# Token factors of the feed-forward's first norm applied to the up projection's outputs, with four leading tiles side by side

## The chip, the cores and the metric

The kernel runs on one core of a Trainium2 chip. The metric is the device time of one execution in microseconds (us). A core has five engines that run their own instruction queues in order: TensorE (PE in the profile, its weight loads PEld), VectorE (DVE), ScalarE (ACT), GpSimd (POOL) and SyncE (SP), which issues the loads from memory. They wait for one another by semaphores. TensorE's results land in PSUM, eight banks of 128 x 512 fp32 numbers; everything else lives in SBUF.

## What is computed

Two layers of a hybrid encoder, all in fp32, on 512 tokens of 1024 channels:

```python
def rms_norm(x, g):
    y = xf * lax.rsqrt(jnp.mean(xf * xf, axis=-1, keepdims=True) + RMS_EPS)
    return y * g
...
for l in range(DEPTH):                      # DEPTH = 2
    h = rms_norm(x, g_pre_mix[l])
    proj = h @ w_in[l]                      # 1024 -> 5632
    ...
    merged = (gates[:, :, 0] * (o_a @ w_br_a[l]) + gates[:, :, 1] * (o_b @ w_br_b[l])
              + gates[:, :, 2] * (o_m @ w_br_m[l]))
    x = x + rms_norm(merged @ w_out[l], g_post_mix[l])
    h = rms_norm(x, g_pre_ffn[l])
    u = depthwise_conv_centred(h @ w_up[l], conv_w[l], conv_b[l])   # 1024 -> 5632, 3 taps over tokens
    a, b = jnp.split(u, 2, axis=-1)
    f = jax.nn.gelu(a) * b
    x = x + rms_norm(f @ w_down[l], g_post_ffn[l])
```

The three attention branches o_a, o_b, o_m (the last one into 256 memory tokens) lie between; the change does not touch them. The norm that matters is the one behind `w_out`: it divides every token by one number, the root of the mean of its squares, and multiplies every channel by g.

## The kernel before

**Layout and precision.** Channels lie on the 128 partitions and tokens along the free axis, so x is eight tiles of 128 x 512 (k = 0 to 7). A product is made as three matmuls of a rounded format (`mm3`): each operand is split into a high part (a cast on ScalarE) and a low part (source minus high part, on VectorE or GpSimd), and high x high, high x low and low x high are summed in PSUM. An output tile of 128 channels takes 8 steps over k of 3 matmuls. It is made at full width (24 matmuls of 512 tokens) or by halves (48 of 256), which lets it begin when only the first 256 tokens of its input are there.

**Weights.** `weights()` loads 512 KB through SP's queue into one of three buffers `wraw`, casts it on ScalarE to `whi` and subtracts on VectorE to `wlo` (two buffers each), or into other pools where the weights have to stay longer. Low parts for which GpSimd is named are made there instead.

**Order.** TensorE's order is written out by hand: the class `Woven` chains every matmul to the one before it and keeps a clock of their estimated cost. Side work (norms, attention heads) stands in generators, the jobs, that are woven in when the clock passes their due time. A job yields a delay or the name of a flag that it waits for; the main line waits with `need` and jobs answer with `give`. The order on the other engines is chosen by the framework's scheduler; each engine then runs its queue in that order.

**The stage of the change.** `sublayer_end` makes the output tiles of `w_out` (and later of `w_down`): each is scaled by g on ScalarE into a tile `og`, and its squares are summed into `acc`. For `w_out` all eight tiles are made by halves. When a token half is complete, `end_job` runs: `rstd_job` multiplies the sums by a vector `mean` on TensorE (the tokens' means land on the partitions), takes the root on ScalarE and the reciprocal on VectorE, builds a diagonal matrix from it on VectorE and multiplies it by a matrix of ones on TensorE, so that every partition of a PSUM tile `pr` holds the 256 factors. Then x is updated, its squares are summed, and `pre_norm_job` does the same a second time for the next norm and makes h = x * g * factor with high and low parts. The flag `h{l}.16.i` says that half i of h is complete.

The up projection has 44 output tiles; tile j and tile j + 22 form a pair. The first six (0, 22, 1, 23, 2, 24) lead: their weights are made ahead, with GpSimd's low parts, and `run_group` computes them by halves, two side by side, in six PSUM banks. The other 38 are made at full width, one after another. `conv` reads the tile from PSUM (ScalarE: middle tap and bias; VectorE: two steps with the other taps), then come GELU, the product of the pair and the split for `w_down`. The casts of the first two single tiles are put behind the last operation of the norm on ScalarE (`fence`).

Between the layers, the last norm of layer 0 and the first of layer 1 run beside the projection of the memory tokens (`mem_kv`). At the start of the program and at its end `rstd_job` has little beside it.

In the profile nearly all operations of ScalarE and VectorE carry line 114 (the helper through which they go), matmuls line 244, transposes 255, GpSimd's low parts 222.

## Time and profile before

| | us |
|---|---|
| median of three runs | 1577.96 (1577.94, 1577.96, 1579.77) |
| the profiled execution | 1579.04 |
| its span, first to last instruction | 1577.3 |
| PE busy | 1529.7 |
| DVE busy | 911.2 |
| ACT busy | 727.4 |
| POOL busy | 186.4 |

The profiled execution is 1.7 us longer than its span: that much lies around the first and last instruction. A row of the timeline gives the start, the time to the end of the last of a group of like instructions, the engine, the line, the operation with its output and inputs, their number, and in brackets the idle time of the engine just before them and what ended it. Matmuls are pipelined, so the time of one is the distance of two starts. A row of windows gives, for a stretch of the span, the busy time of the five engines with the number of instructions, then TensorE's granted clock (1.00 is full speed), the share of the DMA engines and GB/s.

### The profile page before, as it was taken

To read this page: it belongs to the slowest core of one execution; us is meant where nothing else is said; L and a number is where in the kernel's file an instruction comes from. 1 tells how busy PE (TensorE), PEld (TensorE's weight loads), DVE (VectorE), ACT (ScalarE), POOL (GpSimd) and SP (SyncE) were. 2 spreads that over 40 slices of the span, in tenths; PEclk is the share of its full clock that TensorE was granted. 3 is DMA by queue.
4 is the path that set the end of the run, shared out by engine and by line. 5 is a ranking of instruction groups with operands and counts; after the bars stand their busy time and mean duration, and the time that the engine had idled before them with its cause. 6 is when DMAs were issued, how large, how long until landed. Compare 5 with 4: busy or idle time off the path is not lost.

```text
span 1577.3 us, 21375 instructions
## 1 busy us (share of the span) xinstructions
PE 1529.7 (97%) x8246; PEld 1316.4 (83%) x8246; DVE 911.2 (58%) x1654; ACT 727.4 (46%) x1289; POOL 186.4 (12%) x244
## 2 busy tenths in 40 slices
PE   6999999999999999999989999999999999999997
PEld 5988888889898888878888888888898888888887
DVE  6686566344866666542386856743457666664233
ACT  5465575334544444532345646733454544444231
POOL 4340000110400000010062300001121000000000
PEclk9999999999999999999999999999999999999998
DMA  7222213224213222333331221132431232223331
GB/s 241 87 78 67 66 56 100 88 94 134 81 42 106 93 95 96 115 97 100 115 113 49 86 69 56 51 120 74 140 101 48 69 105 95 94 96 96 99 103 62
DMA packets 46614, 144.96 MB, mean 92 GB/s; under 512 B 5232, under 2 KB 11376, under 8 KB 46512
## 3 DMA queue, kind: packets, MB, share of 16 engines
q1 hardware_dynamic: 44656, 139.61, 27.7%
q10 hardware_dynamic: 1152, 2.10, 0.5%
q0 software_dynamic: 704, 1.88, 0.4%
q8 instruction: 65, 1.06, 0.3%
q14 instruction: 37, 0.30, 0.1%
HBM read 141.47 MB, written 2.10 MB: 91 GB/s over the span
## 4 chain that ended last, share of the span: by engine, by line
PE 88%; DVE 8%; ACT 2%; issue 1%; DMA 1%; SPq 0%; ACTq 0%
PE mm L244 73%; PE s L244 6%; PE o L244 3%; PE pt L244 2%; DVE h L114 2%; PE pt L255 2%; DVE y L114 2%; DVE x L114 1%; DVE m L114 1%; DVE wlo L114 1%; ACT whi L114 1%; DVE acc L114 1%; DVE ka L114 0%; ACT y L114 0%; DMA m<-in_memT_dram 0%
## 5 line engine op out<-in xcount | busy, mean ns | idle before, releaser
L244 PE MATMUL mm<-h,whi 128*128 128x512 f32 x2432 | 755.7, 392 | 0.0
L244 PEld LDWEIGHTS mm<-h,whi 128*128 128x128 f32 x2432 | 449.6, 188 | 88.7
L114 DVE TENSOR_TENSOR wlo<-wraw,whi 128x1024 fp32r<-128x1024 f32 (+1 forms) x203 | 246.9, 1218 | 394.9 <-ACT whi L114 394.8
L244 PE MATMUL mm<-h,wlo 128*128 128x512 f32 x1216 | 473.9, 390 | 0.0
L114 ACT CAST whi<-wraw 128x1024 fp32r<-128x1024 f32 (+1 forms) x203 | 210.3, 1038 | 296.5 <-PE mm L244 295.7
L244 PEld LDWEIGHTS mm<-h,wlo 128*128 128x128 f32 x1216 | 228.2, 188 | 48.5
L244 PE MATMUL mm<-m,whi 128*128 128x512 f32 (+1 forms) x672 | 178.2, 354 | 1.6 <-DVE m L114 0.8
L244 PEld LDWEIGHTS mm<-m,whi 128*128 128x128 f32 x672 | 119.6, 192 | 19.0 <-PE mm L244 1.3
L114 DVE SCALAR_TENSOR_TENSOR y<-mm,vec,y 128x511 f32<-128x511 f32 x160 | 118.9, 746 | 8.5 <-ACT y L114 5.9
L244 PE MATMUL mm<-m,wlo 128*128 128x512 f32 (+1 forms) x336 | 118.3, 352 | 0.7 <-DVE wlo L114 0.7
L114 ACT ACTIVATE y<-mm,vec 128x512 f32<-128x512 f32 (+1 forms) x163 | 113.6, 698 | 0.1
L244 PE MATMUL mm<-m,m 128*128 128x512 f32 (+1 forms) x432 | 88.6, 346 | 0.0
L222 POOL TENSOR_TENSOR m<-wraw,m 128x512 fp32r<-128x512 f32 x42 | 56.3, 1355 | 238.5 <-ACT m L114 234.2
L728 POOL TENSOR_TENSOR m<-m,y 128x512 f32<-128x512 f32 x28 | 36.1, 1289 | 405.7 <-DVE y L114 405.7
L244 PEld LDWEIGHTS mm<-m,m 128*128 128x128 f32 x432 | 67.6, 190 | 8.4
L244 PEld LDWEIGHTS mm<-m,wlo 128*128 128x128 f32 x336 | 64.4, 192 | 9.4 <-DVE wlo L114 1.1
L114 ACT ACTIVATE y<-y 128x512 f32<-128x512 f32 x44 | 27.8, 632 | 87.3 <-DVE y L114 87.3
L244 PE MATMUL mm<-h,m 128*128 128x256 f32 x456 | 63.6, 296 | 4.0 <-ACT h L114 1.6
L114 DVE TENSOR_TENSOR acc<-acc,sq 128x256 f32<-128x256 f32 (+1 forms) x86 | 44.6, 521 | 37.5 <-ACT sq L114 36.9
L114 ACT CAST m<-wraw 128x512 fp32r<-128x512 f32 (+1 forms) x98 | 56.1, 602 | 21.1 <-DMA wraw<-in_w_brb_dram 9.5
L244 PEld LDWEIGHTS mm<-h,m 128*128 128x128 f32 x456 | 59.2, 199 | 6.4 <-ACT h L114 2.8
L114 ACT CAST m<-pt 128x512 fp32r<-128x512 f32 (+1 forms) x72 | 38.2, 539 | 40.4 <-PE pt L255 32.0
(150 smaller groups left out, 1835.8 us busy)
## 6 DMA issues: line engine op xcount, KB each, us to landing
wraw<-in_w_in_dram SPq DMA_DIRECT2D x88, 512.0 KB, 3.3
wraw<-in_w_up_dram SPq DMA_DIRECT2D x88, 512.0 KB, 3.3
wraw<-in_w_down_dram SPq DMA_DIRECT2D x32, 512.0 KB, 3.5
wraw<-in_w_out_dram SPq DMA_DIRECT2D x16, 512.0 KB, 3.4
wraw<-in_w_down_dram SPq DMA_DIRECT2D x16, 384.0 KB, 3.1
wraw<-in_w_kv_dram SPq DMA_DIRECT2D x8, 512.0 KB, 3.6
wraw<-in_w_bra_dram SPq DMA_DIRECT2D x16, 192.0 KB, 2.3
x<-in_xT_dram SPq DMA_DIRECT2D x8, 256.0 KB, 7.2
```

Of the source, the lines that this page charges most:

```text
L114: return op(*args, **kw)
L222: last_lo[eng or V] = (eng or V).tensor_sub(lo, src, f32(hi)).ins
L244: wv.pe(nc.tensor.matmul(ps, a, b, start=first, stop=last), cost)
L255: wv.pe(nc.tensor.transpose(ps[:, 128 * i:128 * i + 128], s, ident), 0.11)
L728: (V if br == 2 and m >= 6 else G).tensor_add(acc[m], acc[m], gs)
```

## The change

1. In the feed-forward's first norm the token factors are no longer multiplied into h. `factor_end_job` takes the place of `end_job` and `pre_norm_job` there: as x is updated, `raw_split` makes high and low parts of x * g, with one flag per k, for which `run_group` waits. The factors are made afterwards and kept in a tile R (128 x 512); `scaled` multiplies each of the 44 up tiles by R on VectorE, and the convolution reads the result from SBUF. Pairs finished before R is there are held: at the third pair the main line waits for R.
2. Four up tiles lead (0, 22, 1, 23) instead of six, and all four go side by side, k by k.
3. Four of the eight tiles of `w_out` are made at full width instead of none. The leading up tiles' weights are made during these.
4. `rstd_job` has no diagonal and no ones: the factors, as an operand that repeats one column, are multiplied by the identity, 128 tokens at a time.
5. `end_job` waits for the estimated end of ScalarE's and VectorE's work before its mean, and before the next norm.
6. The low parts of the leading weights, of `w_up`, of the memory projection and of layer 1's `w_in`, move from GpSimd to VectorE.
7. Two pools become one (32 and 16 tiles become 48), and one kind of small tile has three buffers instead of four.

```diff
-SQG, LOG, GEN, KVE = {0: (), 1: ()}, {0: (), 1: ()}, 'GGVGVG', 'VVGG'
+SQG, LOG, GEN, KVE = {0: (), 1: ()}, {0: (), 1: ()}, 'VVVVVV', 'VVVV'
...
-    mp = ctx.enter_context(tc.tile_pool(name="mp", bufs=32))
-    hp = ctx.enter_context(tc.tile_pool(name="hp", bufs=16))
+    mp = ctx.enter_context(tc.tile_pool(name="mp", bufs=48))
...
         V.reciprocal(rs, rs)
-        diag = small("h32", 4, (128, n))
+        yield 0.8
         for b in range(nb):
-            V.tensor_scalar_mul(diag[:, 128 * b:128 * b + 128], ident, rs[:, b:b + 1])
-        yield 1.2
-        mm(pr, ones, diag, True, True, n * 4 / 2400.0)
+            one = rs[:, b:b + 1]
+            spread = bass.AP(one.tensor, one.offset, [list(one.ap[0]), [0, 128]])
+            mm(pr[:, 128 * b:128 * b + 128], spread, ident, True, True, 0.22)
...
+    def raw_split(l, goff, k, src, hi, lo):
+        g = vec[:, l, goff + k:goff + k + 1]
+        ACT.activation(hi, src, AF.Copy, scale=g)
+        V.scalar_tensor_tensor(out=lo, in0=src, scalar=g, in1=f32(hi), op0=ALU.mult, op1=ALU.subtract)
...
+    def scaled(ps, R):
+        y = ytile()
+        V.tensor_mul(y, ps, R)
+        return y
...
     def end_job(l, goff, og, acc, acc2, i, then, lat, more=()):
-        yield lat
+        yield ready(lat)
...
-            yield 9.0
+            yield ready(1.0)
...
+    def factor_end_job(l, goff, og, acc, acc2, i, nxt):
+        half, box = HALVES[i], []
+        gnext, h, R = nxt
+        yield ready(1.4)
+        yield from rstd_job([acc[:, half]], 256, box)
+        for k in range(KD):
+            V.tensor_mul(og[k][:, half], og[k][:, half], box[0])
+            V.tensor_add(x[k][:, half], x[k][:, half], og[k][:, half])
+            raw_split(l, gnext, k, x[k][:, half], h[k][0][:, half], h[k][1][:, half])
+            if k == 0:
+                yield 0.6
+            wv.give(f"h{l}.{gnext}.{i}.{k}")
+            yield 1.05
+        for k in range(KD):
+            sumsq_add(acc2[:, half], x[k][:, half], k == 0)
+        yield ready(1.0)
+        box = []
+        yield from rstd_job([acc2[:, half]], 256, box)
+        ACT.copy(R[:, half], box[0])
+        if i == 1:
+            yield 0.6
+            wv.give(f"R{l}.{gnext}")
...
-    def conv(l, m, ps):
-        y = ytile()
+    def conv(l, m, ps, R):
+        u, y = scaled(ps, R), ytile()
...
-        up = (0, 22, 1, 23, 2, 24)
-        sublayer_end(l, V_POST, lambda m, i: [lambda: weights(w_out[l, m], KD, 128, WOUT[min(i, 4)])],
-                     ms, 8, lambda a, i, l=l, hs=hs: pre_norm_job(l, V_PREF, a, hs, i))
-        gw = group_weights([w_up[l, m] for m in up], (G,) * 6)
+        up = (0, 22, 1, 23)
+        sublayer_end(l, V_POST, lambda m, i: [lambda: weights(w_out[l, m], KD, 128, None if i in (None, 3) else ktile)],
+                     ms, 4, (V_PREF, hs, R), fill=[lambda m=m: gw.extend(group_weights([w_up[l, m]], (V,))) for m in up])
+        pss = dict(zip(up, (sbank(), sbank(), obank(128), mmbank())))
...
+            held.append((j, pair))
+            if j >= 2:
+                wv.need(f"R{l}.{V_PREF}")
+            while held and f"R{l}.{V_PREF}" in wv.flags:
+                mixed(*held.pop(0))
```

How the queues move, at three places. First, TensorE in layer 0 after the change, at the end of the leading group (`o` and `mm` are its last two banks, `mm_4419` is the first single up tile, `pt_4407` the bank of the second norm's half 1, `ident` with `st_4410` the spread of its factors):

```order
L238 MATMUL o_4112<-m_3617,m_3762 128x256
L238 MATMUL mm_4113<-m_3617,m_3806 128x256
L238 MATMUL mm_4113<-m_3618,m_3806 128x256
L238 MATMUL mm_4113<-m_3617,m_3807 128x256
L238 MATMUL pt_4407<-mean,acc_3631 128x1 x2
L238 MATMUL mm_4419<-m_3603,whi_4415 128x512
L238 MATMUL mm_4419<-m_3604,whi_4415 128x512
L238 MATMUL mm_4419<-m_3603,wlo_4416 128x512
```

On ScalarE the cast of that tile's weights stands directly behind the root:

```order
L114 ACTIVATE sq_892_4368<-x_83 128x256
L114 ACTIVATE st_4410<-pt_4407,eps 128x2
L114 CAST whi_4415<-wraw_4413 128x1024
L114 CAST whi_4449<-wraw_4447 128x1024
L114 COPY R_3619<-pt_4407 128x256
L114 ACTIVATE y_4480<-y_4478,vec 128x512
```

Before, on the same engine at the same place, eight casts of h stood between the root and the cast of the first single tile's weights, which came after the group's own mean and spread had been woven into the middle of the group:

```order
L114 ACTIVATE st_4507<-pt_4504,eps 128x2
L114 CAST h_3614<-h_934_4526 128x256
L114 CAST h_3616<-h_935_4530 128x256
L114 CAST h_3618<-h_936_4534 128x256
L114 CAST h_3620<-h_937_4538 128x256
L114 CAST h_3622<-h_938_4542 128x256
L114 CAST h_3624<-h_939_4546 128x256
L114 CAST h_3626<-h_940_4550 128x256
L114 CAST h_3628<-h_941_4554 128x256
L114 CAST whi_4752<-wraw_4750 128x1024
```

So the mean, which stood in the group's half 1, stands at its end now, and the root with it.

Second, VectorE in layer 0 after the change, where the third single tile (the first of the fourth pair) gets its weights' low part, `wlo_4535`. `mm_4419` and `mm_4453` are the outputs of the two single tiles before it, `R_3619` holds the token factors, and the twenty rows from `y_4478` on, of which these are the last eleven, belong to the three held pairs:

```order
L114 TENSOR_TENSOR y_4480<-y_4480,y_4486 128x512
L114 SCALAR_TENSOR_TENSOR y_4504<-y_4502,vec,y_4504 128x511
L114 TENSOR_TENSOR y_4514<-mm_4419,R_3619 128x512
L114 TENSOR_TENSOR m_4493<-y_4480,m_4492 128x512
L114 SCALAR_TENSOR_TENSOR y_4504<-y_4502,vec,y_4504 128x511
L114 SCALAR_TENSOR_TENSOR y_4516<-y_4514,vec,y_4516 128x511
L114 TENSOR_TENSOR y_4498<-y_4498,y_4504 128x512
L114 SCALAR_TENSOR_TENSOR y_4516<-y_4514,vec,y_4516 128x511
L114 TENSOR_TENSOR y_4520<-mm_4453,R_3619 128x512
L114 TENSOR_TENSOR m_4511<-y_4498,m_4510 128x512
L114 TENSOR_TENSOR wlo_4535<-wraw_4532,whi_4534 128x1024
```

Before, the low parts of the first two single tiles stood ahead of all convolution steps:

```order
L114 TENSOR_TENSOR h_3627<-h_940_4550,h_3626 128x256
L114 TENSOR_TENSOR h_3629<-h_941_4554,h_3628 128x256
L114 TENSOR_TENSOR wlo_4753<-wraw_4750,whi_4752 128x1024
L114 TENSOR_TENSOR wlo_4788<-wraw_4785,whi_4787 128x1024
L114 SCALAR_TENSOR_TENSOR y_4708<-mm_4324,vec,y_4708 128x511
L114 SCALAR_TENSOR_TENSOR y_4712<-mm_4325,vec,y_4712 128x511
L114 SCALAR_TENSOR_TENSOR y_4708<-mm_4324,vec,y_4708 128x511
L114 SCALAR_TENSOR_TENSOR y_4712<-mm_4325,vec,y_4712 128x511
L114 TENSOR_TENSOR y_4708<-y_4708,y_4712 128x512
L114 SCALAR_TENSOR_TENSOR y_4722<-s_4326,vec,y_4722 128x511
L114 SCALAR_TENSOR_TENSOR y_4726<-s_4327,vec,y_4726 128x511
```

What moved: the low part of a later tile's weights stands behind all the held pairs' work, and each tile has a multiply by R of its own ahead of its convolution.

Third, ScalarE between the layers. `m_7185` is the copy of the memory projection's third tile (its values), which TensorE transposes into `s_7203`; the casts ahead of it are high parts of h for layer 1. After:

```order
L114 CAST m_7116<-mm_7069 64x256
L114 CAST m_7088<-h_1383_7132 128x256
L114 CAST m_7090<-h_1384_7136 128x256
L114 CAST m_7092<-h_1385_7140 128x256
L114 CAST m_7094<-h_1386_7144 128x256
L114 CAST m_7096<-h_1387_7148 128x256
L114 CAST m_7098<-h_1388_7152 128x256
L114 CAST m_7100<-h_1389_7156 128x256
L114 CAST m_7102<-h_1390_7160 128x256
L114 COPY m_7185<-mm_7126 128x256
L114 CAST m_7206<-s_7203 128x4x64
L114 COPY m_7218<-mm_7187 128x256
```

Before:

```order
L114 CAST m_7240<-mm_7215 64x256
L114 CAST h_7254<-h_1381_7292 128x256
L114 COPY m_7333<-mm_7250 128x256
L114 CAST h_7256<-h_1382_7296 128x256
L114 CAST h_7258<-h_1383_7300 128x256
L114 CAST h_7260<-h_1384_7304 128x256
L114 CAST m_7354<-s_7351 128x4x64
```

The copy, which stood behind one cast of h, stands behind eight.

## The prediction

> **What bounds the kernel now.** I read the page first, then the clock by stage, then TensorE's timeline around each stop, and last the ScalarE and VectorE rows that end those stops. From the page, the busy shares and the chain that ended last:

> ```profile
> PE 1529.7 (97%) x8246; PEld 1316.4 (83%) x8246; DVE 911.2 (58%) x1654; ACT 727.4 (46%) x1289; POOL 186.4 (12%) x244
> ...
> PE 88%; DVE 8%; ACT 2%; issue 1%; DMA 1%; SPq 0%; ACTq 0%
> ```

> TensorE is the bound. A change can win only by giving it cheaper matmuls or by removing stops, and whatever is late next costs in full. The place is the front of the feed-forward: from the first output matmul of `w_out` to the first up tile that is computed alone. TensorE's timeline in layer 0 (start, length, group, count, idle before it and what ended that):

> ```profile
> 369.05 0.51 PE L244 MATMUL mm<-m,ka 128*128 128x256 f32 x3
> ...
> 383.27 3.04 PE L244 MATMUL s<-m,m 128*128 128x256 f32 x24
> 386.15 1.12 PE L244 MATMUL mm<-m,m 128*128 128x256 f32 x8
> ...
> 409.29 0.58 PE L244 MATMUL pt<-mean,acc 128*128 128x1 f32 x4 [2.32 <-DVE acc L114]
> ...
> 412.88 0.67 PE L244 MATMUL pt<-h,ones 128*128 128x256 f32 x2 [1.47 <-DVE h L114]
> ...
> 437.11 0.50 PE L244 MATMUL pt<-mean,acc 128*128 128x1 f32 x4
> ...
> 440.59 0.39 PE L244 MATMUL mm<-h,m 128*128 128x256 f32 x1 [0.30 <-ACT h L114]
> 441.27 0.86 PE L244 MATMUL mm<-h,m 128*128 128x256 f32 x5 [0.30 <-DVE h L114]
> ...
> 458.55 0.63 PE L244 MATMUL mm<-h,whi 128*128 128x512 f32 x2
> ```

> This front takes 458.55 - 369.05 = 89.50 us. It holds 14 tiles by halves (8 of `w_out`, 6 of the up projection). 24 half-width matmuls take 386.15 - 383.27 = 2.88 us, 0.12 each, so a tile of 48 takes 5.76 us and the 14 take 80.6. Of the other 8.9 us, 2.32 + 1.47 + 0.30 + 0.30 = 4.4 are stops and 4.5 the four pairs of mean and spread matmuls with the slow restarts about them. The two long stops belong to the norm: the sum of squares of the new x, then the diagonal matrix.

> The same front in layer 1, and a full-width stretch:

> ```profile
> 1144.70 0.52 PE L244 MATMUL mm<-m,ka 128*128 128x256 f32 x3
> ...
> 1185.02 0.58 PE L244 MATMUL pt<-mean,acc 128*128 128x1 f32 x4 [2.32 <-DVE acc L114]
> ...
> 1188.61 1.19 PE L244 MATMUL pt<-h,ones 128*128 128x256 f32 x2 [0.89 <-DVE h L114]
> ...
> 1236.36 0.63 PE L244 MATMUL mm<-h,whi 128*128 128x512 f32 x2
> ```
> ```profile
> 640.82 0.61 PE L244 MATMUL mm<-h,whi 128*128 128x512 f32 x2
> ...
> 641.50 0.61 PE L244 MATMUL mm<-h,whi 128*128 128x512 f32 x2
> ```

> Layer 1 takes 1236.36 - 1144.70 = 91.66 us, 2.16 more, though its second stop is shorter. The granted clock says why. Four windows by engine; the first is round the 2.32-us stop of layer 0, the second round the stop of 3.04 us between the layers (quoted below), the others behind the 2.32-us stop of layer 1; the third figure from the right is the clock:

> ```profile
> 406.00:412.00 6.00, 3.08 (x25) 2.70 (x23) 4.78 (x11) 4.51 (x13) 2.17 (x2) 1.00 0.27 87
> 809.00:815.00 6.00, 2.96 (x24) 2.73 (x23) 5.70 (x11) 2.61 (x6) 2.48 (x2) 1.00 0.51 168
> 1184.00:1192.00 8.00, 6.09 (x30) 5.67 (x31) 5.74 (x15) 4.43 (x13) 1.27 (x1) 0.64 0.21 68
> 1192.00:1200.00 8.00, 8.00 (x65) 8.00 (x65) 6.29 (x14) 5.99 (x16) 2.29 (x2) 0.93 0.00 0
> ```

> So a stop between 2.3 and 3.1 us sometimes costs the clock and sometimes does not. Where it did, 8 x 0.36 + 8 x 0.07 = 3.4 us of clock were missing, and the front came out 2.16 us longer.

> **The change, part by part.** *Fewer tiles by halves.* At full width three matmuls take 641.50 - 640.82 = 0.68 us, so a tile of 24 takes 5.44. The new front is the same 14 tiles: four of `w_out` at full width, four by halves, four leading up tiles by halves, two more at full width: 6 x 5.44 + 8 x 5.76 = 78.7 us, 1.9 less than 80.6. This is certain, and it is the whole gain in matmul time.

> *The old stops.* For the rest I need ScalarE's rows and VectorE's rows in this front:

> ```profile
> 437.65 0.26 ACT L114 ACTIVATE st<-pt,eps 128x2 f32<-128x2 f32 x1 [3.52 <-PE pt L244]
> 440.13 1.19 ACT L114 CAST h<-h 128x256 fp32r<-128x256 f32 x3 [2.22 <-DVE h L114]
> ...
> 450.69 1.28 ACT L114 ACT_TABLE_LOAD   x1 [2.15 <-DVE y L114]
> ...
> 469.43 1.05 ACT L114 CAST whi<-wraw 128x1024 fp32r<-128x1024 f32 x1 [0.95 <-PE mm L244]
> ```
> ```profile
> 342.68 0.68 DVE L114 TENSOR_TENSOR y<-mm,y 128x512 f32<-128x512 f32 x1
> ```
> ```profile
> 438.14 0.48 DVE L114 TENSOR_SCALAR h<-ident,st 128x128 f32<-128x128 f32 x2
> 439.62 1.26 DVE L114 SCALAR_TENSOR_TENSOR h<-x,vec,pt 128x256 f32<-128x256 f32 x3 [0.99 <-PE pt L244]
> ...
> 460.54 0.74 DVE L114 SCALAR_TENSOR_TENSOR y<-o,vec,y 128x511 f32<-128x511 f32 x1
> 461.20 0.74 DVE L114 SCALAR_TENSOR_TENSOR y<-pt,vec,y 128x511 f32<-128x511 f32 x1
> ...
> 470.52 1.22 DVE L114 TENSOR_TENSOR wlo<-wraw,whi 128x1024 fp32r<-128x1024 f32 x1 [2.77 <-ACT whi L114]
> ...
> 475.96 1.23 DVE L114 TENSOR_TENSOR wlo<-wraw,whi 128x1024 fp32r<-128x1024 f32 x1 [0.66 <-ACT whi L114]
> ```

> Half 0 of h now needs, per k, a multiply, an add and one split operation on VectorE, at no more than 1.26 / 3 = 0.42 each: 1.3 us per k, 10 for all eight. TensorE has four half tiles of `w_out`, 4 x 2.88 = 11.5 us, to do meanwhile, and then takes 12 x 0.12 = 1.44 us per k, so it doesn't overtake. For half 1 the cover is the group's half 0, again 11.5 us. I therefore take all 4.4 us of stops as gone; the 4.5 us of pairs and restarts stay near 4.0, since the number of pairs is unchanged and new stops restart too (3.4 to 4.5). The price if this cover fails is a rival below.

> *New stop one: the end of the leading group.* The mean matmul of half 1 stands there, and behind it the first tile whose weights are made in passing. Their cast is queued on ScalarE behind the square root. From a mean at 437.11 the root started 0.54 later and took 0.26; then the cast takes 1.05 and the low part 1.22. TensorE, 0.4 past the mean's start, waits 0.54 + 0.26 + 1.05 - 0.4 = 1.5 us for the cast, computes two matmuls, and waits about 0.75 more for the low part: 2.3 us. The bounds are 1.5 and 2.7.

> *New stop two: the first tile of the fourth pair.* No output of the three held pairs may go on before R exists. Counting T from the end of the leading group: the root ends at 0.8, the low part at 3.2, the spread follows six matmuls into the tile, and R is copied at about T + 5.1. On VectorE twenty operations of the held pairs (six multiplies by R, ten steps of the convolution, four of gate and split) then stand ahead of the low part of that tile's weights. One follows another at 461.20 - 460.54 = 0.66 us: 20 x 0.66 = 13.2, and with the low part's 1.22 the chain ends at T + 19.5, or 19.1 since the shorter multiplies take less. The table load of 1.28 lies beside it. TensorE is there at T + 0.4 + 2.3 + 2 x 5.44 + 0.8 (spread and two matmuls) = T + 14.4. It waits 4.7 us. The floor is 2.7: the multiply by R of the tile just finished (0.68), one split step (0.68) and the low part (1.22) stand in that order behind the tile's own end, with the handoffs. The ceiling is 5.5.

> The front after is 78.7 + 4.0 + 2.3 + 4.7 = 89.7 us in each layer: +0.2 in layer 0, -2.0 in layer 1, together -1.8.

> *The rest of the up loop.* 38 multiplies by R at 0.68 add 26 us to VectorE in this stretch of layer 0:

> ```profile
> 458.55:672.90 214.35, 213.08 (x940) 175.79 (x938) 132.31 (x160) 96.65 (x129) 5.33 (x6) 1.00 0.29 96
> ```

> 132 + 26 = 158 of 214 us; before each low part VectorE had 2.77 or 0.66 us idle, which takes one multiply of 0.68. I cost it at nothing; without that cover it would be up to 26 us per layer, which the 56 us left speak against. The splits moved from GpSimd to VectorE for the leading tiles, eight per layer, lie under the 21.8 us of `w_out`'s full tiles; their loads on SP only go out earlier.

> *The turn between the layers.* TensorE's rows there:

> ```profile
> 787.61 0.67 PE L244 MATMUL pt<-h,ones 128*128 128x256 f32 x2 [1.27 <-DVE h L114]
> ...
> 798.98 0.62 PE L244 MATMUL mm<-h,m 128*128 128x256 f32 x3 [0.65 <-ACT y L114]
> ...
> 812.65 0.67 PE L244 MATMUL pt<-h,ones 128*128 128x256 f32 x2 [3.04 <-DVE h L114]
> ...
> 817.38 5.63 PE L244 MATMUL s<-h,m 128*128 128x256 f32 x45 [0.83 <-DVE m L114]
> ```

> I take these four, 5.8 us, as gone. In their place ScalarE's copy of the memory values is queued behind eight casts of h instead of one, 8 x 0.40 = 3.2 us, and the transposes on TensorE behind it wait about 3.1; the last norm's mean and spread now stand at the end of a group and wait some 2.2 (0 to 3.5). Net -0.5, with bounds of -5 and +2.5.

> *Start and end.* The diagonal's 0.48 us goes from both chains:

> ```profile
> 12.90 1.19 PE L244 MATMUL pt<-h,ones 128*128 128x256 f32 x2 [1.16 <-DVE h L114]
> ```
> ```profile
> 1568.34 0.99 PE L244 MATMUL pt<-h,ones 128*128 128x256 f32 x2 [1.16 <-DVE h L114]
> ```

> -0.5 at each end. The sum without the clock is -1.8 - 0.5 - 1.0 = -3.3 us.

> *The clock.* A stop of 2.32 us lost the clock once in two; none of 4.7 is among those shown. I take it to lose the clock in both layers, at the 2.16 us by which layer 1 was longer (1.7 to 3.4): +4.3. The transition's 3.1 us I leave at full clock, like the 3.04 us before.

> [...]

> **How the numbers follow.** The profiled execution took 1579.04 us, 1.08 above the median of 1577.96. The sum is -3.3 + 4.3 = +1.0 us: 1580.0 for such an execution, 1579.0 for the median. A measurement of this kernel tells about 0.2%, 3.2 us, from no change, so "same" is 1574.8 to 1581.1.

> **The rivals.** *Forecast* (0.42): both new stops as costed, the clock lost twice; 1579.0.

> *The second new stop is near its floor and the clock stays* (0.31): VectorE begins the held work sooner and the stop is 2.7 us. Then -3.3 - 2 x 2.0 = -7.3: 1570.7. If the stop stays at 4.7 and only the clock holds, it is -3.3: 1574.7; half of the 0.31 is for that. For it: 3.04 us at full clock; against it: twenty operations counted in the order of the program.

> *The clock is what decides* (0.20): it is lost at the two 4.7-us stops and at the 3.1-us stop between the layers, each at 3.4 us as in the windows. Then -3.3 + 10.2 = +6.9: 1584.9, slower. It is slower once three drops cost over 2.2 us each.

> *The change doesn't remove the old stops* (0.07): h comes later than counted and 2.32 us remain in each layer, +4.6: 1583.6, slower.

> Faster by over 0.2% gets 0.31, within 0.42, slower 0.27. The range reaches from 1570.5 to 1584.5.

> **What would show it.** Right: no stop at the mean of `w_out`; a stop of about 2.3 us (cast, then low part) at the first single up tile; one of 4 to 5.5 us ended by a low part, two tiles later, at the fourth pair; a clock of 0.6 to 0.7 in the 8 us behind it; and the COPY behind eight casts at the turn. Wrong: the fourth pair starts without a stop over 3 us, or a full clock behind it, or VectorE's idle time ahead of low parts gone through the whole up loop.

## The result, and the profile after

| | median us | range, runs |
|---|---|---|
| before, beside it | 1579.31 | 1577.94 to 1583.48, 5 |
| changed | 1584.84 | 1582.92 to 1586.72, 5 |

The ratio is 1.0032, with a 95% interval of 1.0017 to 1.0048: slower by about 5 us. By the bound of 0.2% in the prediction that is "slower", to which it gave 0.27; "same" at 1579.0 had 0.42. The interval's lower end lies just under that bound. The prediction counted its times and its range (1570.5 to 1584.5) from a median of 1577.96 for the kernel before; beside the changed kernel that median was 1579.31. On the prediction's scale the ratio gives 1577.96 x 1.0032 = 1583.0 us, inside the range, near its upper end. The profiled execution took 1584.93 us with a span of 1583.1, 5.8 more than before.

The page of the changed kernel, first line of the busy shares:

```profile
PE 1531.8 (97%) x7994; PEld 1307.1 (83%) x7994; DVE 948.8 (60%) x1694; ACT 735.8 (46%) x1267; POOL 138.5 (9%) x207
```

TensorE has 252 fewer matmuls, should need 3.8 us less for them (1.9 per layer by the prediction's count), and is busy for 2.1 us longer. So the matmuls became slower, and the clock is the place to look. First the stops of TensorE that bear on the argument, from its timeline, with the rows that mark the stages (a bracket holds the idle time before a row):

```profile
366.67 0.61 PE L238 MATMUL mm<-m,whi 128*128 128x512 f32 x2
...
438.43 0.73 PE L238 MATMUL mm<-m,whi 128*128 128x512 f32 x2 [1.28 <-ACT whi L114]
439.69 0.64 PE L238 MATMUL mm<-m,wlo 128*128 128x512 f32 x1 [0.53 <-DVE wlo L114]
...
457.56 0.79 PE L238 MATMUL mm<-m,wlo 128*128 128x512 f32 x1 [4.62 <-DVE wlo L114]
...
674.27 0.73 PE L238 MATMUL mm<-m,whi 128*128 128x512 f32 x2 [1.82 <-ACT whi L114]
676.20 0.80 PE L238 MATMUL mm<-m,wlo 128*128 128x512 f32 x1 [1.19 <-DVE wlo L114]
...
811.53 0.44 PE L249 MATMUL s<-ident,m 128*128 128x128 f32 x2 [3.27 <-ACT m L114]
...
1152.29 0.62 PE L238 MATMUL mm<-m,whi 128*128 128x512 f32 x2
...
1224.25 0.73 PE L238 MATMUL mm<-m,whi 128*128 128x512 f32 x2 [1.28 <-ACT whi L114]
1225.51 0.50 PE L238 MATMUL mm<-m,wlo 128*128 128x512 f32 x1 [0.53 <-DVE wlo L114]
...
1241.81 0.63 PE L238 MATMUL mm<-m,wlo 128*128 128x512 f32 x1 [4.63 <-DVE wlo L114]
...
1574.44 0.71 PE L238 MATMUL pt<-ident,st 128*128 128x128 f32 x4 [0.55 <-DVE st L114]
```

The stops at `acc` and `h` (2.32, 1.47, 0.30, 0.30) are gone, and the two new ones are there in both layers: 1.81 us in two parts at the first single up tile, 4.62 us at the first tile of the fourth pair. The row at 674.27 is a third, at the first tile of `w_down` in layer 0. Before, TensorE's timeline at the same place read:

```profile
671.55 0.73 PE L244 MATMUL mm<-m,whi 128*128 128x512 f32 x2 [0.65 <-ACT whi L114]
672.96 0.50 PE L244 MATMUL mm<-m,wlo 128*128 128x512 f32 x1 [0.68 <-DVE wlo L114]
```

Windows round these stops; the clock is the third figure from the right:

```profile
438.00:446.00 8.00, 7.05 (x25) 5.52 (x26) 5.45 (x7) 3.92 (x6) 0.00 (x0) 0.79 0.39 132
454.00:458.00 4.00, 0.44 (x1) 0.44 (x2) 4.00 (x6) 1.98 (x3) 0.00 (x0) 0.87 0.01 2
458.00:466.00 8.00, 8.00 (x24) 6.26 (x24) 3.58 (x6) 1.08 (x2) 0.00 (x0) 0.64 0.44 131
675.00:683.00 8.00, 6.81 (x19) 5.36 (x19) 2.54 (x2) 0.00 (x0) 1.65 (x2) 0.57 0.42 118
811.00:816.00 5.00, 4.47 (x26) 4.47 (x26) 2.07 (x5) 2.75 (x7) 0.00 (x0) 0.66 0.00 0
1222.00:1230.00 8.00, 6.19 (x34) 4.93 (x33) 4.93 (x7) 4.20 (x7) 0.00 (x0) 1.00 0.38 121
1240.00:1248.00 8.00, 6.19 (x20) 4.96 (x21) 5.59 (x8) 1.49 (x3) 0.00 (x0) 0.79 0.41 131
```

Before, one stop up to the last spread lost the clock; now five do: both of 4.6 us, layer 0's first stop (layer 1's like one at 1224 does not), the one at `w_down` and the one at the turn. From these windows 1.7 + 0.5 + 2.9 + 3.4 + 1.7 + 1.7 = 11.9 us of clock are missing (the length of a window times what its clock lacks to 1.00), against 3.4 before.

By stage, from the starts in the rows of both kernels (a stage that ends at a stop is counted to the idle time's start; the front's end is put 0.45 us, two matmuls, before the end of the stop at the fourth pair):

| stage | before | after | difference | forecast |
|---|---|---|---|---|
| start to layer 0's `w_out` | 369.05 | 366.67 | -2.4 | -0.5 |
| front of layer 0 | 89.5 | 90.4 | +0.9 | +0.2 |
| up loop to `w_down` | 212.3 | 215.3 | +3.0 | +2.2 |
| `w_down`, turn, attention to layer 1's `w_out` | 473.8 | 479.8 | +6.0 | -0.5 |
| front of layer 1 | 91.7 | 89.1 | -2.6 | -2.0 |
| to the last spread | 332.0 | 333.1 | +1.1 | +1.7 |
| end | 9.0 | 8.7 | -0.3 | |

(The last forecast is 2.2 for the clock and -0.5 for the end.) All rows but the first and the fourth came out within 1 us. The fourth is the one that decides.

### The profile page after: what moved, and what is told of

Its sections match the earlier page's. It is cut to its first block, busy times and chain, and to the rows that moved or that the text cites. A ratio compares the mean times of both kernels' runs of the same rounds, so it can differ in the third digit from the quotient of the medians.

```text
span 1583.1 us, 20671 instructions
## 1 busy us (share of the span) xinstructions
PE 1531.8 (97%) x7994; PEld 1307.1 (83%) x7994; DVE 948.8 (60%) x1694; ACT 735.8 (46%) x1267; POOL 138.5 (9%) x207
## 4 chain that ended last, share of the span: by engine, by line
PE 52%; DVE 3%; ACT 1%; issue 1%; DVEq 0%; ACTq 0%
PE mm L238 46%; PE s L238 2%; PE o L238 2%; PE pt L249 1%; DVE m L114 1%; DVE y L114 1%; PE pt L238 1%; DVE wlo L114 0%; DVE x L114 0%; DVE h L114 0%; ACT m L114 0%; DVE ka L114 0%; DVE acc L114 0%; ACT L114 0%; ACT whi L114 0%
## 5 line engine op out<-in xcount | busy, mean ns | idle before, releaser
L238 PE MATMUL mm<-m,whi 128*128 128x512 f32 (+1 forms) x3296 | 996.8, 385 | 5.3 <-ACT whi L114 4.4
L238 PEld LDWEIGHTS mm<-m,whi 128*128 128x128 f32 x3296 | 607.3, 189 | 120.1 <-ACT whi L114 5.0
L238 PE MATMUL mm<-m,wlo 128*128 128x512 f32 (+1 forms) x1648 | 632.7, 384 | 11.5 <-DVE wlo L114 11.5
L114 DVE TENSOR_TENSOR wlo<-wraw,whi 128x1024 fp32r<-128x1024 f32 (+1 forms) x213 | 259.5, 1220 | 294.5 <-ACT whi L114 292.0
L238 PEld LDWEIGHTS mm<-m,wlo 128*128 128x128 f32 x1648 | 311.8, 189 | 74.8 <-DVE wlo L114 13.7
L114 ACT CAST whi<-wraw 128x1024 fp32r<-128x1024 f32 (+1 forms) x213 | 220.7, 1039 | 317.9 <-PE mm L238 309.7
L238 PE MATMUL mm<-m,m 128*128 128x256 f32 (+1 forms) x720 | 133.6, 328 | 4.2 <-DVE m L114 2.1
L114 DVE SCALAR_TENSOR_TENSOR y<-y,vec,y 128x511 f32<-128x511 f32 x176 | 131.2, 750 | 3.6 <-ACT y L114 0.9
L114 DVE TENSOR_TENSOR y<-mm,R 128x512 f32<-128x512 f32 x82 | 56.4, 688 | 78.5 <-PE mm L238 78.5
L238 PE MATMUL o<-m,m 128*128 128x256 f32 (+2 forms) x448 | 74.4, 291 | 1.2 <-DVE m L114 1.2
L238 PE MATMUL s<-m,m 128*128 128x256 f32 (+2 forms) x480 | 71.5, 292 | 3.5 <-DVE st L114 1.6
L114 ACT ACTIVATE y<-y,vec 128x512 f32<-128x512 f32 x88 | 71.2, 813 | 2.9 <-DVE y L114 2.7
L114 DVE TENSOR_TENSOR m<-wraw,m 128x512 fp32r<-128x512 f32 (+1 forms) x80 | 51.0, 660 | 33.1 <-ACT m L114 32.9
L238 PEld LDWEIGHTS s<-m,m 128*128 128x128 f32 x480 | 63.8, 191 | 7.9 <-DVE st L114 3.5
L114 ACT ACTIVATE y<-y 128x512 f32<-128x512 f32 x44 | 27.8, 632 | 75.6 <-DVE y L114 75.3
L114 ACT CAST m<-wraw 128x512 fp32r<-128x512 f32 (+1 forms) x86 | 47.8, 592 | 27.5 <-DMA wraw<-in_w_down_dram 9.7
L114 DVE TENSOR_TENSOR acc<-acc,sq 128x256 f32<-128x256 f32 (+1 forms) x80 | 38.7, 484 | 33.0 <-ACT sq L114 30.9
L114 ACT CAST m<-y 128x512 fp32r<-128x512 f32 x32 | 19.8, 619 | 81.2 <-DVE y L114 81.2
L114 ACT ACTIVATE y<-mm,vec 128x512 f32<-128x512 f32 (+1 forms) x91 | 57.4, 630 | 0.1
```

What stands on the lines that cost most here:

```text
L114: return op(*args, **kw)
L238: wv.pe(nc.tensor.matmul(ps, a, b, start=first, stop=last), cost)
```

## The experiments

Two theories. A: the loss is made of TensorE's stops and of the half clock behind them. B: the 44 multiplies by R per layer are too much for VectorE, and the stops only show where this comes to light first. The kernel before had a median of 1579.1 to 1579.6 us beside each set of runs, 12 to 23 runs each.

| kernel | median us | ratio to before | 95% interval |
|---|---|---|---|
| changed | 1584.84 | 1.0032 | 1.0017 to 1.0048 |
| 1: fourth pair's first weights ahead | 1574.33 | 0.9963 | 0.9950 to 0.9976 |
| 2: no fence | 1579.43 | 0.9999 | 0.9990 to 1.0007 |
| 3: both | 1568.29 | 0.9930 | 0.9918 to 0.9943 |
| 4: memory squares on VectorE | 1579.50 | 0.9999 | 0.9991 to 1.0008 |
| 5: before, with the new spread | 1576.60 | 0.9980 | 0.9971 to 0.9989 |
| 6: three repairs (1, 2 and 4) | 1562.28 | 0.9888 | 0.9875 to 0.9902 |
| 7: 6, values first | 1566.46 | 0.9913 | 0.9900 to 0.9927 |
| 8: 6, multiply twice | 1563.04 | 0.9897 | 0.9882 to 0.9911 |
| 9: 6, `w_out` all by halves | 1575.42 | 0.9975 | 0.9964 to 0.9985 |
| 10: before, new spread and squares | 1574.66 | 0.9965 | 0.9952 to 0.9977 |
| 11: 6, low parts on GpSimd | 1565.74 | 0.9909 | 0.9896 to 0.9923 |
| 12: 6, both tiles of the pair ahead | 1560.06 | 0.9876 | 0.9860 to 0.9891 |

**1. The second new stop.** In the changed kernel, the weights of the fourth pair's first tile are asked for before the held pairs' work:

```diff
-        fs, fence, n, held = [], crit[0], 0, []
+        fs, fence, n, held, early = [], crit[0], 0, [], []
...
-                    w = weights(w_up[l, m], KD, 128, after=fence if n <= 2 else None)
+                    w = early.pop(0) if early else weights(w_up[l, m], KD, 128, after=fence if n <= 2 else None)
...
+            if j == 2:
+                early.append(weights(w_up[l, 3], KD, 128))
             if j >= 2:
                 wv.need(f"R{l}.{V_PREF}")
```

> The weights of the fourth pair's first tile are made ahead of the held pairs' work. Theory A (the loss is made of TensorE's stops and of the half clock behind them): the stop of 4.62 us goes in both layers (-9.2 us), and of the 23.9 us at half clock 6.8 + 3.4 go, worth about 5: 12 to 14 us less than the changed kernel, near 1571. Theory B (the 44 multiplies by R per layer are too much for VectorE, and the stop is only where it shows first): the stop moves on to the next low parts, and less than 3 us come back, 1582 to 1585.

It came out 10.5 us under the changed kernel. The stop at the first tile went, and one came at the pair's second tile, whose low part now stands behind the held work. TensorE's timeline of this kernel:

```profile
459.54 0.50 PE L238 MATMUL mm<-m,wlo 128*128 128x512 f32 x1 [1.67 <-DVE wlo L114]
...
1238.59 0.50 PE L238 MATMUL mm<-m,wlo 128*128 128x512 f32 x1 [1.67 <-DVE wlo L114]
```

So 2 x 2.95 = 5.9 us of stops went instead of 9.2, and these 3.3 us cover what is short of 12 to 14. Theory B's "less than 3 us" is out.

**2. The first new stop.** `after=fence if n <= 2 else None` became `after=None`.

> The casts of the first two single tiles may run ahead of the root. Theory A: the stop of 1.28 + 0.53 us goes in both layers (-3.6) and with it layer 0's first 3.4 us at half clock (-1.7): about 1579.5; the stop of 4.6 stays. Theory B: nothing, since VectorE has the same work, 1583 to 1586.

1579.43, as theory A had it. The stop of 1.81 us is gone in both layers, and 4.58 us remain at the fourth pair.

**3. Both edits.**

> Both edits. Theory A: -9.2 - 3.6 of stops and 13.7 us at half clock less (-6.8), together 17 to 20: near 1566, faster than the kernel before. Theory B: 1580 to 1585, with stops spread over the up loop.

1568.29, 16.6 us under the changed kernel, a little less than forecast, since twice 1.63 us remain at the fourth pair. In the profiled execution (1564.54, mean granted clock 0.998 against 0.990 in the changed kernel's) the clock is never lost between the start and the end.

**4. The stop at `w_down`.** `MSQ = G` became `MSQ = V`: in layer 1's norm of the memory tokens the squares are summed on VectorE. ScalarE's rows in the changed kernel:

```profile
668.80 1.67 ACT L114 ACTIVATE sq<-m 128x256 f32<-128x256 f32 x5
671.20 0.42 ACT L114 ACTIVATE sq<-m 128x256 f32<-128x256 f32 x1 [0.72 <-POOL h L312]
672.34 0.42 ACT L114 ACTIVATE sq<-m 128x256 f32<-128x256 f32 x1 [0.73 <-POOL h L312]
672.66 0.60 ACT L114 CAST ka<-y 128x512 fp32r<-128x512 f32 x1
673.17 1.78 ACT L114 CAST whi<-wraw 128x1024 fp32r<-128x1024 f32 x2
```

The last pair's split (`ka`) could have begun earlier: its product `y` was ready at 670.60 + 1.11 = 671.71, as VectorE's row shows:

```profile
670.60 1.11 DVE L114 TENSOR_TENSOR y<-y,y 128x512 f32<-128x512 f32 x1
```

The first cast of `w_down`'s weights, and the split ahead of it, stand behind two squares that wait for GpSimd to free their buffers, 1.45 us in all. That made the split, and the cast behind it, about 0.95 us late (672.66 against 671.71); the stop at the cast grew by 1.17 us, from 0.65 to 1.82. In the kernel before, ScalarE's rows there were:

```profile
666.69 1.68 ACT L114 ACTIVATE sq<-h 128x256 f32<-128x256 f32 x5
669.31 0.62 ACT L114 CAST ka<-y 128x512 fp32r<-128x512 f32 x1 [0.94 <-DVE y L114]
669.84 0.72 ACT L114 ACTIVATE sq<-h 128x256 f32<-128x256 f32 x2
670.47 1.76 ACT L114 CAST whi<-wraw 128x1024 fp32r<-128x1024 f32 x2
```

The split stood ahead of the last two squares, and by their time GpSimd was far enough.

> Layer 1's squares of the memory tokens are summed on VectorE instead of GpSimd. If ScalarE's queue there waits for GpSimd (its squares stand ahead of the last split of the up loop), the stops of 1.82 + 1.19 us at w_down fall to about 1.3 in all, as before the change, and the 6.8 us at half clock behind them go: 5 us less, near 1580. If the stop comes of the multiply by R in the last pair, it stays at 3.0 and the time at 1584.

1579.50, as forecast. (Its profiled execution took 1574.86 us, the fastest of eleven.) ScalarE's rows of this kernel at the same place:

```profile
666.47 1.63 ACT L114 ACTIVATE sq<-m 128x256 f32<-128x256 f32 x5
668.00 1.04 ACT L114 CAST whi<-wraw 128x1024 fp32r<-128x1024 f32 x1
669.00 0.63 ACT L114 CAST ka<-y 128x512 fp32r<-128x512 f32 x1
669.54 0.71 ACT L114 ACTIVATE sq<-m 128x256 f32<-128x256 f32 x2
```

TensorE has no stop left here, not even the 1.33 us of the kernel before. The last pair is multiplied by R as before the edit, so the multiply alone doesn't make the stop; layer 1, where the last pair has the same multiply, has no stop there in the changed kernel either. The edit did two things at once: nothing waits for GpSimd, and the scheduler put the cast ahead of the last split and the last squares. Which of them is worth how much of the 3.0 us was not separated.

**5. The spread alone, in the kernel before.** The diagonal and `ones` of `rstd_job` replaced as in the change, nothing else.

> The kernel before with one part of the change, the spread of the factors by the identity in place of the diagonal and ones. Theory A: the diagonal's 0.5 us and the queue it stands in go from every norm on the path: -1.1 at the first stop of the program, -0.6 at the end, the stops of 1.27, 3.04 and 1.47 us at x's second norm shrink; 4 to 7 us less than before, 1572 to 1575. Theory B says nothing of it; if the matmuls of one repeated column are slow, the time stays within 1 us of before.

1576.60: 2.9 us less, short of 4 to 7. At a mark in the start (the matmul that waits 0.84 us for a low part) this kernel's profile stands at 63.66 us, the kernel before at 65.18 and the changed one at 62.78. In the eleven profiles of kernels that start as the changed one does it lies between 62.67 and 64.72, so how much of the 1.5 us is the edit can't be read from one profile each. The stops of the norms were not removed, they moved to the next thing late. TensorE's timeline of this kernel, and the row of VectorE that ended the second stop:

```profile
407.80 0.73 PE L244 MATMUL pt<-mean,acc 128*128 128x1 f32 x4 [2.67 <-DVE acc L114]
...
816.50 3.86 PE L244 MATMUL s<-h,m 128*128 128x256 f32 x21 [4.02 <-DVE m L114]
```
```profile
815.94 0.41 DVE L114 TENSOR_TENSOR m<-s,m 128x256 fp32r<-128x256 f32 x1
```

2.67 us instead of 2.32 + 1.47 in layer 0, and at the turn 4.02 us instead of 3.04 at the diagonal. This stop is not at h, with which three matmuls of the same group had begun: it ended when VectorE had split the transposed memory values (`m<-s,m`), which stood in a bank of the kind `s`, as the group's next tile needs.

**6. The three repairs together.**

> The changed kernel with the three edits of the first runs together (weights ahead at the fourth pair, no fence, memory squares on VectorE). Theory A: the stop of 3.0 us at w_down goes too, and no stop but the one of 3.3 us at the turn is left to lose the clock: 3 to 5 us less than with two edits, 1563 to 1566, ratio 0.990 to 0.992. If VectorE's load decides, no better than 1568.

1562.28: 22.6 us under the changed kernel and 17 under the one before, a little better than forecast. Of TensorE's waits in this kernel the largest inside the program are these (total, times, longest):

```profile
PE s L249 <- ACT m L114: 3.3, 1, 3.3
PE mm L238 <- DVE wlo L114: 3.2, 2, 1.6
```

**7. The turn.** In layer 1 `for m in range(4)` of the memory projection became `for m in (2, 3, 0, 1)`.

> The same, and in layer 1 the memory projection makes its two value tiles ahead of its two key tiles, so that ScalarE's copy stands ahead of the casts of h. If the 3.3-us stop at the turn comes of the copy behind eight casts, it shrinks to the second copy's (under 2 us) and the time falls by 1 to 3 us against the three repairs; if it is h itself that is late, PE waits as long at h and the time stays.

A miss: 4.2 us slower. ScalarE's rows of this kernel:

```profile
787.64 0.38 ACT L114 COPY m<-mm 128x256 f32<-128x256 f32 x1
...
791.54 1.19 ACT L114 CAST m<-h 128x256 fp32r<-128x256 f32 x3 [2.39 <-DVE h L114]
...
796.29 0.41 ACT L114 CAST m<-h 128x256 fp32r<-128x256 f32 x1 [0.32 <-DVE h L114]
796.61 0.36 ACT L114 COPY m<-mm 128x256 f32<-128x256 f32 x1
```

The first copy came ahead of the casts, but the second fell behind all eight, and TensorE stopped 1.78 us at the first and 3.22 at the second. That a copy queued behind the casts of h makes the stop fits these rows; how to remove it was not found.

**8. The multiply by R, doubled.** For the pairs 4 to 19 a second `V.tensor_mul(u, ps, R)` writes the same product again.

> The three repairs, and the multiply by R is done twice for the 32 up tiles of pairs 4 to 19 of each layer (64 operations more, 40 us of VectorE). Theory A (the multiply is hidden in the up loop): within 2 us of the three repairs. Theory B: 10 to 40 us slower.

1563.04, 0.8 us from the three repairs, though VectorE is busy for 37 us more (982.1 against 945.1). The multiply is hidden in the up loop, and theory B falls.

**9. The width of `w_out`'s tiles.** Its eight tiles by halves again, the leading up weights made behind them:

```diff
-        sublayer_end(l, V_POST, lambda m, i: [lambda: weights(w_out[l, m], KD, 128, None if i in (None, 3) else ktile)],
-                     ms, 4, (V_PREF, hs, R), fill=[lambda m=m: gw.extend(group_weights([w_up[l, m]], (V,))) for m in up])
+        WOUT = (ktile, ktile, None, None, big)
+        sublayer_end(l, V_POST, lambda m, i: [lambda: weights(w_out[l, m], KD, 128, WOUT[min(i, 4)])],
+                     ms, 8, (V_PREF, hs, R))
+        gw.extend(group_weights([w_up[l, m] for m in up], (V,) * 4))
```

> The three repairs with the output projection's eight tiles all by halves again (part 3 of the change undone). Theory A: four tiles per layer at 5.76 instead of 5.44 us, 8 x 0.32 = 2.6 us slower than the three repairs, near 1565; more if the first halves of x*g then come late. If width does not matter, within 1 us.

1575.42, 13.1 us slower than the three repairs where 2.6 were forecast. TensorE's timeline of this kernel:

```profile
411.23 0.58 PE L238 MATMUL pt<-mean,acc 128*128 128x1 f32 x4 [0.98 <-DVE acc L114]
...
461.57 0.50 PE L238 MATMUL mm<-m,wlo 128*128 128x512 f32 x1 [3.16 <-DVE wlo L114]
```

A stop at the sums of squares is back (0.98 and 0.92 us in the two layers), and the one at the fourth pair is 3.16 instead of 1.62, in both layers. Together that is 2.6 + 1.9 + 3.1 = 7.6 us. The clock was lost behind both 3.16-us stops, for 3.4 us at half speed each, 1.7 us of clock: 11.0 in all. The rest of the 13 is not accounted for row by row. The edit did several things: narrower tiles, other buffers for their weights, and the leading weights later. The width of the matmuls is worth 2.6; which of them brings the stops was not separated.

**10. What needs no token factors.** The kernel before with the new spread and the squares on VectorE.

> The kernel before with the new spread and the memory squares on VectorE, that is, the parts that need no token factors. It tells what the factors themselves bring: theory A: the stop of 1.3 us at w_down goes and the rest stays as in the run of the spread alone, 1574 to 1576, so that the factors, the leading four and the full-width tiles are worth 11 to 14 us of the three repairs' gain. The rival, that the gain of the three repairs is the squares' and the spread's, wants 1565 or less.

1574.66, as forecast. So 12.4 of the 17 us that the three repairs have over the kernel before come with the rest of the change (the factors, the leading four, the wider tiles, the low parts moved to VectorE, the new waits), once its stops are out of the way. Run 11 undoes a part of it; the others were not taken apart.

**11. Low parts on GpSimd.** In the three repairs, `'VVVVVV', 'VVVV'` set back to `'GGVGVG', 'VVGG'`.

> The three repairs with the low parts of the memory projection and of layer 1's first weights back on GpSimd in part (part 6 undone there). Theory A: VectorE has that work beside others at the turn; if GpSimd slows VectorE's operations there as in the kernel before (2.35 us for a pair of 0.48), the stops at the turn grow, 1 to 4 us slower; if not, 0 to 2 us faster.

1565.74, 3.5 us slower, as forecast: at the turn TensorE stops for 2.80 us at `acc` and 4.02 us at the split of the memory values, where the three repairs have 3.26 us at the copy and 1.07 at that split. Beside the three repairs, that part of the change is a gain.

**12. Both tiles of the fourth pair ahead.**

```diff
-                early.append(weights(w_up[l, 3], KD, 128))
+                early.append(weights(w_up[l, 3], KD, 128, big))
+                early.append(weights(w_up[l, 25], KD, 128, big))
```

> The three repairs with both tiles of the fourth pair prepared ahead, into buffers of the large pool, so that their low parts wait for no tile before them. Theory A: the rest of the second new stop, 1.62 us in each layer, goes: 3 us less, near 1559, ratio 0.987. If the stop moves on to the fifth pair, no gain.

1560.06: no stop over 0.2 us is left between layer 0's `w_out` and the turn, and this is the best time of the study, 1.2% under the kernel before and 1.6% under the changed one. Against the three repairs the median fell by 2.2 us, with overlapping intervals.

## Why the prediction was right and wrong

**The old stops** went, as forecast, in both layers. **The new stops** are where the order of the program put them and about as long as worked out: 1.81 us for 2.3, and 4.62 and 4.63 for 4.7. The sum of twenty operations at 0.66 us each on VectorE was good to 0.1 us. **The fronts** came out at 90.4 and 89.1 us for 89.7. That layer 0's is so near is partly luck: it holds 1.7 us of lost clock that the sum did not have.

**The clock** was lost behind both 4.6-us stops. The missing clock there was 3.4 us in layer 0 (0.5 + 2.9) and 1.7 in layer 1, for 2.16 each. It was lost once more behind the first stop of layer 0, which I had left out: 1.7 us. It was lost at the turn too, which I had left at full clock: 1.7 us. That it was lost at the first stop, at `w_down` and at the turn is in part the luck of this execution, as the last section shows.

**The step that failed** is "The rest of the up loop", "I cost it at nothing". It holds inside the loop, as the doubled multiply shows. It does not hold at the loop's end in layer 0: all the squares of the memory tokens now stand ahead of the last pair's split and of `w_down`'s first cast on ScalarE, and two of them wait there for GpSimd. (Why the scheduler put them there was not shown; the last pair's later product is the likely reason.) Stops grew from 1.33 to 3.01 us, and behind them 3.4 us of clock were missing: 5.1 us, while the sum fell short by 4.8 (5.8 measured on the span, 1.0 forecast). Moving these squares gave 5.3 us back. In layer 1, which has no memory norm behind it, neither kernel stops there.

**The start** gained 2.4 us where I had 0.5. A part of that is not the change: the first matmul came 0.9 us earlier (8.97 against 9.90), and run 5 gives the scatter of the start. **The turn** got the stop at the copy as forecast (3.27 us for 3.1), and 0.55 + 1.01 + 0.30 us at the last norm for 2.2. But of the four old stops that I took as gone the last stayed, 1.07 us for 0.83, because it waits for the memory values (run 5) and not for the norm. So the turn's stops came to 6.2 us where I had 5.3.

**The rivals.** That the second stop would be near its floor was wrong: 4.62. So was the other half of that rival, that the clock holds behind a stop of this length: it was lost in both layers. The third rival had the side right and half the mechanism: what decides is the clock, lost five times where it named three, with a price of 1.7 to 3.4 us each. It gave 6.9 us more than before; 5 were measured.

## What to carry to other kernels

A stop costs its length and then, perhaps, the clock: the three repairs took 2 x (1.8 + 4.6 - 1.6) + 3.0 = 12.6 us of stops away and returned 22.6. When work is held back until a late result, list everything that will stand ahead of the next weights in each in-order queue, and ask for those weights before the held work. And follow a small delay past the end of its loop: what comes next on the same queue may be work for another stage, waiting for an engine that the loop never used.

## What was not expected of the hardware

Some stops lost the clock every time, some at times, some never. Over the profiled executions of this study: stops of 4.6 us lost it six times in six (the changed kernel and those of runs 2 and 4), of 2.67 us four in four (the kernels of runs 5 and 10), of 3.16 two in two (run 9), the 3.3-us stop at the turn five in nine, the 1.82 + 1.19 us at `w_down` two in four, 1.28 + 0.53 us once in six, 1.6 us never in twelve. Shorter stops at the turn lost it too: 1.78 us in run 7, 1.43 in run 5, and a stretch round a stop of 1.01 us in runs 1, 7, 9 and 12. How long the half clock lasted follows from the changed kernel's windows: (0.13 x 4 + 0.36 x 8) / 0.5 = 6.8 us at half clock behind 457 us and 0.21 x 8 / 0.5 = 3.4 us behind 438 and behind 1241.

```profile
404.61:408.02 3.41, 2.36 (x20) 2.16 (x18) 3.41 (x6) 1.34 (x3) 1.90 (x2) 1.00 0.48 154
408.02:411.44 3.42, 2.11 (x16) 1.94 (x16) 2.24 (x7) 3.17 (x11) 0.26 (x1) 1.00 0.00 0
...
1182.85:1186.26 3.41, 1.24 (x11) 1.27 (x12) 2.84 (x6) 2.42 (x9) 0.78 (x1) 1.00 0.22 89
1186.26:1189.67 3.41, 2.52 (x11) 2.08 (x10) 1.89 (x5) 1.38 (x5) 1.27 (x1) 0.50 0.14 25
```

The 3.3-us stop at the turn, in the changed kernel (3.00 us idle in one stretch, lost) and in that of run 3 (1.74 and 1.52 us in two, kept):

```profile
808.53:811.94 3.41, 0.41 (x4) 0.41 (x5) 2.88 (x8) 1.96 (x5) 0.00 (x0) 1.00 0.00 0
811.94:815.35 3.41, 3.41 (x19) 3.41 (x18) 0.99 (x2) 1.86 (x5) 0.00 (x0) 0.50 0.00 0
```
```profile
794.39:797.80 3.41, 1.67 (x14) 1.47 (x13) 3.41 (x11) 2.06 (x6) 0.45 (x2) 1.00 0.12 46
797.80:801.21 3.41, 1.89 (x16) 1.89 (x17) 1.82 (x5) 1.83 (x6) 0.00 (x0) 1.00 0.00 0
```

In the traces of the kernel before and the changed one, cut into such stretches from 100 us to the last spread, all five at full clock with TensorE idle for 2.17 to 3.41 us lost it, one of the eight with 1.28 to 1.86 us did (1.81, ahead of the fall at 439.88), and none with less. What tells the one from the seven is not shown, nor what makes the clock fall. The mean granted clock of one kernel differs from one execution to the next (0.991 to 0.996 in the twelve of the kernel before beside runs 9 to 12), so a median holds the mean of lucky and unlucky stops.
